# VectorE makes 12 of 16 k-tiles of the modulation sums for norm 1's last three k-tiles, in a backbone-layer kernel on one core

## The chip, the cores and the metric

The kernel runs on one core of one Trainium2 chip. TensorE (PE in the profile, PEld its weight loads) multiplies into PSUM; VectorE (DVE) and ScalarE (ACT) work on SBUF and PSUM; SyncE (SP) issues most DMAs. The metric is the device time of one execution in microseconds (us), lower is better; times are medians of runs on the chip.

## What is computed

One layer over 128 context tokens and 256 latent tokens, all in float32, with d = 2048: modulation vectors from two conditioning vectors, an RMS norm that they scale and shift, an input projection, attention and a Fourier branch, gates, an output projection, and a SwiGLU feed-forward part behind a second norm. Only the start matters here:

```python
def modulation(cond, w_mod, b_mod):
    m = jax.nn.silu(cond) @ w_mod + b_mod
    return jnp.split(m[..., None, :], 6, axis=-1)
...
    sh1, sc1, g1, sh2, sc2, g2 = modulation(cond, w_mod_l, b_mod_l)
    h = rms_norm(x, n1) * (1 + sc1) + sh1
    q, k, v, u = project_in(h, w_in_l, qg_l, kg_l)
```

`w_mod` is 2048 x 12288. Each of sh1 and sc1 is, for each of the two conditions, a sum over 2048 rows of the weight, that is over 16 k-tiles of 128 rows. The other four (g1, sh2, sc2, g2) are needed later.

## The kernel before

**Tiles and units.** Large products are made in float32r as three products of high and low halves (`mm3`, lines 146 to 149). Weights come in units of 256 x 512, loaded by SyncE into `wraw` (four buffers) and split into `wh` by ScalarE and `wl` by VectorE (`split`, lines 142 to 144). `next_unit` (208) splits a unit two ahead of the one that TensorE multiplies, and calls the paced side work in the lists `front` and `behind`: each `Paced` object (58) adds its `rate` to `due` at every unit and, once `due` reaches `least`, runs so many steps of its generator.

**The input projection** runs over k-tiles in four groups, `GROUPS` = (0, 1), (1, 2), (3, 4), (7, 9) (first k-tile, count), each over eight column blocks, so that multiplying can begin as soon as the first normed k-tile is there. A unit of the groups with 2 or 4 k-tiles is 18 products of 128 x 512 on TensorE; at the end of a block VectorE adds three PSUM tiles to `acc` (line 682). The 8 units of the group (1, 2) are called the second group below.

**The modulation of norm 1** is made for output k-tiles in groups, `MODS` = (0, 1), (1, 3), (4, 3), (7, 3), (10, 3), (13, 3). For a group of three, `mod_sums` (392) has 8 steps of two k-tiles of `w_mod`: four matmuls of 128 x 32 by 128 x 384 in plain float32, which lie in four column groups of the array (line 404), from `wm` tiles with four buffers (`mod_weights`, 376). In the trace each such matmul stands as two records, so a step is 8 records. Behind the last step ScalarE copies the sums to `mrow` (412), and `mod_cols` (416) turns them to columns by three small matmuls with `sel` (420) and three VectorE additions. Then `modulate` (535) makes h for one k-tile per step. `prepare` (570) runs the next group's sums with the steps behind the last group's sums in between (`next(follow, None)`, 577), at rates `PREP` = 1.75, 1.8, 1.8, 1.8 and `least` 3.6, that is, in bursts of three or four steps every second unit.

**The other modulation vectors** are made by VectorE alone (`mod_rows`, 306): two conditions times 16 k-tiles of `scalar_tensor_tensor` over 128 x 1024 (line 329), then a matmul with `ones` that adds up the partitions (338) into one of the four `at` buffers of PSUM, and an addition of the bias (343). This side work (`rows`) begins when `prepare` ends (`prep.then = with_rows`, 605) and goes on at fixed rates per unit through all later stages, to the feed-forward part. Attention's transposes (862, 865, 960), score and value products take their PSUM tiles from the same four `at` buffers in turn.

**Order.** The kernel runs under a manual schedule: each engine executes its instructions in the order in which the code emits them, and waits where a tile or a buffer is not ready.

Of the kernel before, what the change touches and what calls it, by code (L numbers as in the profile page):

```python
# [13 lines left out]
F32 = mybir.dt.float32  # L14
F32R = mybir.dt.float32r
AF = mybir.ActivationFunctionType
ALU = mybir.AluOpType
AX = mybir.AxisListType

P = 128  # L20
D = 2048
KT = D // P
# [17 lines left out]
GROUPS = [(0, 1), (1, 2), (3, 4), (7, 9)]  # L40
ORDER = [6, 7, 0, 1, 2, 3, 4, 5]
DUE = [-1.4, 0, 0, 0]
PREP = [1.75, 1.8, 1.8, 1.8]
PAIR = "t1 qk,b,,,,lq,s0 s1 m0,e0 i0,m1,pv lb,e1 i1,,t0,v,lv"


# [55 lines left out]
def trunk_kernel(ctx: ExitStack, tc: tile.TileContext, io: dict):  # L102
# [35 lines left out]
    def nm(s):  # L138
        return f"{s}{next(ids)}"
# [126 lines left out]
    with ExitStack() as ph:  # L266
# [22 lines left out]


        ROWS = (2, 4, 3, 5)

        def row_weights():

# [77 lines left out]
        def depth_of(n):  # L372

            return 4 if n == 1 else 2

        def mod_weights(alloc):


            def load(kt0, n, k0):
                w, nk = n * P, depth_of(n)  # L380
                wm = alloc([P, 2, nk, w], "wm")
                for ty in range(2):
                    col = ty * D + kt0 * P
                    nc.sync.dma_start(
                        wm[:, ty],
                        w_mod[k0 * P : (k0 + nk) * P, col : col + w].rearrange("(k p) n -> p k n", p=P),
                    )
                return wm

            return Ahead(load, [(kt0, n, k0) for kt0, n in MODS for k0 in range(0, KT, depth_of(n))], 0)  # L390

        def mod_sums(src, kt0, n, alloc, out):

# [3 lines left out]
            for k0 in range(0, KT, nk):  # L397
                _, wm = src.take()
                for kk in range(0, nk, 2):
# [13 lines left out]
                        out.append(rows)  # L413
                    yield

        def mod_cols(kt0, n, rows):

            pt = md_tile()
            for j in range(n):
                nc.tensor.matmul(pt[:, j * 4 : j * 4 + 4], rows[:, j * P : (j + 1) * P], sel, start=True, stop=True)  # L420
            m = pt[:, : n * 4].rearrange("p (k i c) -> p k i c", i=2, c=2)
            yield


            def bc(ap):
                return ap.unsqueeze(2).to_broadcast([P, n, 2])

            nc.vector.tensor_add(msh[0][:, kt0 : kt0 + n, :], m[:, :, 0], bc(bcol[:, kt0 : kt0 + n]))
            d = msc[0][:, kt0 : kt0 + n, :]
            nc.vector.tensor_add(d, m[:, :, 1], bc(bcol[:, KT + kt0 : KT + kt0 + n]))  # L430
            nc.vector.scalar_tensor_tensor(
                out=d, in0=d, scalar=1.0, in1=bc(ng[:, 0, kt0 : kt0 + n]), op0=ALU.add, op1=ALU.mult
            )
            yield


        with ExitStack() as pha:
            wmp = phm.enter_context(tc.tile_pool(name="wmp", bufs=4, side="right"))
            cpool = pha.enter_context(tc.tile_pool(name="cpool", bufs=12))
            tmp = pha.enter_context(tc.tile_pool(name="tmpa", bufs=2))  # L440

# [128 lines left out]
            def prepare():  # L570

                follow = columns_and_tokens(*MODS[0])
                while prepared[0] < 1:
                    yield next(follow)
                for k0, n in MODS[1:]:
                    for _ in mod_sums(src, k0, n, wme, sums):
                        next(follow, None)
                        yield
                    follow = columns_and_tokens(k0, n)
                    while k0 == 1 and prepared[0] < 3:  # L580
                        yield next(follow)
                for _ in follow:
                    yield

            prep = Paced(prepare())
            rows_psum["tile"] = md_tile

            def rows_and_columns():
# [62 lines left out]

            for gi, (k0, n) in enumerate(GROUPS):
                prep.due, prep.rate = DUE[gi], PREP[gi]
                prep.least = 3.6 if gi else 1
                if gi == len(GROUPS) - 1:
                    behind.append(Paced(expand_rpb(), 0.2))
                    new_ring()
# [755 lines left out]
```

## Time and profile before

| what | us |
|---|---|
| median of 3 runs | 2045.73 (2045.72 to 2048.85) |
| profiled execution, device time | 2046.09 |
| its span, first to last instruction | 2044.3 |
| TensorE busy in the span | 2022.1 |
| VectorE busy in the span | 1244.4 |

The span leaves out about 1.8 us around the instructions. TensorE's busy time is the union of its records, which overlap; idle time before a record stands in brackets in the views of the timeline, with what ended it. A wait that the profile names is put down to the semaphore that came last.

### The profile page before, as it was taken

What the parts mean: (1) busy time and instruction counts of PE and PEld (TensorE: products, weight loads), DVE (VectorE), ACT (ScalarE), POOL (GpSimd) and SP (SyncE); (2) the same over time, 40 slices, a digit from 0 to 9 for tenths busy, and PEclk for the clock granted to TensorE, in tenths of its full rate; (3) what the DMA queues carried; (4) which work ended last, traced back from release to release, by engine and by line L of the source; (5) the groups of instructions that cost most, each with busy time, mean ns of one, the idle gap of its engine ahead of it and who ended that gap; (6) DMA issues with size and microseconds to landing.
All of it is one profiled execution on the core that took longest, in us unless ns stands there. A gap on an engine that the chain in (4) does not pass through costs nothing.

```text
span 2044.3 us, 27532 instructions
## 1 busy us (share of the span) xinstructions
PE 2022.1 (99%) x10986; PEld 1844.3 (90%) x10986; DVE 1244.4 (61%) x1524; ACT 758.6 (37%) x1139; POOL 43.0 (2%) x92
## 2 busy tenths in 40 slices
PE   7999999999999999999999999999999999999999
PEld 4668888999999999889998999899989998999897
DVE  4746898778988778765844454544454334333456
ACT  5433232456656443334523332222322232323222
POOL 1000000000000000010000000000000000000000
PEclk8999999999999999999999999999999999999999
DMA  9995979677776776754455455444554444444453
GB/s 328 334 338 181 330 261 323 206 224 225 230 209 185 251 245 200 240 189 139 120 169 162 147 156 160 148 155 148 162 155 141 124 127 125 132 124 125 138 161 124
DMA packets 220384, 390.46 MB, mean 191 GB/s; under 512 B 28464, under 2 KB 77632, under 8 KB 220256
## 3 DMA queue, kind: packets, MB, share of 16 engines
q1 hardware_dynamic: 213088, 382.13, 59.5%
q10 hardware_dynamic: 4672, 6.31, 0.8%
q8 instruction: 86, 1.41, 0.3%
q0 software_dynamic: 2496, 0.27, 0.1%
q14 instruction: 42, 0.34, 0.0%
HBM read 371.81 MB, written 20.51 MB: 192 GB/s over the span
## 4 chain that ended last, share of the span: by engine, by line
PE 93%; DMA 3%; DVE 2%; ACT 1%; issue 0%; SPq 0%; ACTq 0%; DVEq 0%
PE mm L147 19%; PE mm L149 19%; PE mm L148 19%; PE at L147 11%; PE at L149 11%; PE at L148 11%; PE at L404 1%; DVE wl L144 1%; DMA wm<-in_w_mod 1%; DMA wraw<-in_w_in 1%; DVE accr L329 1%; DMA xc<-in_x_prompt 0%; PE at L981 0%; PE at L960 0%; PE at L338 0%
## 5 line engine op out<-in xcount | busy, mean ns | idle before, releaser
L144 DVE TENSOR_TENSOR wl<-wraw,wh 128x1024 fp32r<-128x1024 f32 (+1 forms) x464 | 559.1, 1205 | 672.7 <-ACT wh L143 668.9
L143 ACT CAST wh<-wraw 128x1024 fp32r<-128x1024 f32 (+1 forms) x464 | 481.1, 1038 | 1036.8 <-PE at L148 274.1
L147 PE MATMUL mm<-hH,wh 128*128 128x384 f32 x1152 | 387.9, 337 | 0.2 <-ACT gst L1036 0.2
L149 PE MATMUL mm<-hH,wl 128*128 128x384 f32 x1152 | 385.3, 334 | 0.0
L148 PE MATMUL mm<-hL,wh 128*128 128x384 f32 x1152 | 385.2, 334 | 0.0
L329 DVE SCALAR_TENSOR_TENSOR accr<-wmr,csz,accr 128x1024 f32<-128x1024 f32 x240 | 304.2, 1278 | 0.1
L147 PEld LDWEIGHTS mm<-hH,wh 128*128 128x128 f32 x1152 | 216.3, 188 | 5.1 <-issue 4.5
L148 PEld LDWEIGHTS mm<-hL,wh 128*128 128x128 f32 x1152 | 216.3, 188 | 0.0
L149 PEld LDWEIGHTS mm<-hH,wl 128*128 128x128 f32 x1152 | 216.2, 188 | 0.0
L147 PE MATMUL at<-hH,wh 128*128 128x384 f32 x640 | 213.9, 334 | 0.0
L149 PE MATMUL at<-hH,wl 128*128 128x384 f32 x640 | 213.9, 334 | 0.0
L148 PE MATMUL at<-hL,wh 128*128 128x384 f32 x640 | 213.8, 334 | 0.0
L147 PE MATMUL mm<-wh,hH 128*128 128x512 f32 x404 | 160.8, 398 | 1.9 <-ACT hH L548 1.2
L149 PE MATMUL mm<-wh,hL 128*128 128x512 f32 x404 | 158.4, 392 | 0.6 <-DVE hL L144 0.4
L148 PE MATMUL mm<-wl,hH 128*128 128x512 f32 x404 | 158.0, 391 | 0.8 <-DVE wl L144 0.8
L149 PE MATMUL mm<-wh,cL 128*128 128x512 f32 x352 | 137.1, 389 | 0.0
L147 PE MATMUL mm<-wh,cH 128*128 128x512 f32 x352 | 137.0, 389 | 0.0
L148 PE MATMUL mm<-wl,cH 128*128 128x512 f32 x352 | 137.0, 389 | 0.0
L147 PEld LDWEIGHTS at<-hH,wh 128*128 128x128 f32 x640 | 120.1, 188 | 1.0 <-ACT wh L143 0.8
L148 PEld LDWEIGHTS at<-hL,wh 128*128 128x128 f32 x640 | 120.1, 188 | 0.2
L149 PEld LDWEIGHTS at<-hH,wl 128*128 128x128 f32 x640 | 120.1, 188 | 0.0
L147 PEld LDWEIGHTS mm<-wh,hH 128*128 128x128 f32 x404 | 76.1, 188 | 25.6 <-issue 3.1
(282 smaller groups left out, 2631.1 us busy)
## 6 DMA issues: line engine op xcount, KB each, us to landing
wraw<-in_w_gate_up SPq DMA_DIRECT2D x176, 512.0 KB, 3.7
wmr<-in_w_mod SPq DMA_DIRECT2D x128, 512.0 KB, 4.9
wraw<-in_w_down SPq DMA_DIRECT2D x88, 512.0 KB, 3.7
wraw<-in_w_gate SPq DMA_DIRECT2D x64, 512.0 KB, 4.3
wm<-in_w_mod SPq DMA_DIRECT2D x80, 384.0 KB, 6.8
wraw<-in_w_in SPq DMA_DIRECT2D x56, 512.0 KB, 6.2
wraw<-in_w_o SPq DMA_DIRECT2D x32, 512.0 KB, 4.6
wraw<-in_w_fnet_proj SPq DMA_DIRECT2D x16, 512.0 KB, 5.0
```

Source lines behind the costliest of these rows:

```text
L143: nc.scalar.copy(H, x)
L144: nc.vector.tensor_sub(L, x, fr(H))
L147: nc.tensor.matmul(out, aH, bH, start=start, stop=False)
L148: nc.tensor.matmul(out, aH, bL, start=False, stop=False)
L149: nc.tensor.matmul(out, aL, bH, start=False, stop=stop)
L329: nc.vector.scalar_tensor_tensor(out=acc[:, cnd], in0=wm, scalar=sc, in1=acc[:, cnd], op0=ALU.mult, op1=ALU.add)
L404: nc.tensor.matmul(pm[q : q + 32, :w], csz[:, k, :], wm[:, ty, kk + par, :], start=k < 2, stop=k >= KT - 2, tile_position=(0, q), skip_gro ...
```

## The change

For the last group, (13, 3), the first four k-tiles (`EARLY` = 4) are still multiplied by TensorE. The other 12 k-tiles are multiplied and summed by VectorE in the new generator `late_sums`: for each k-tile and each of shift and scale one load of 128 x 384 (`wd`, five buffers) and two VectorE instructions over 128 x 384, one per condition, into four accumulators that lie in buffers of later h tiles. It is paced at `LATE` = 1.5 steps per unit from the second group of the projection on. `late_rows` then makes on TensorE the two remaining steps of sums and four matmuls with `hot`, which add the accumulators' partitions into the same PSUM tile. The steps behind the sums of (10, 3) no longer have the sums of (13, 3) in between: they come one after the other. The rates in the last two groups go from 1.8 to 1.6, and `least` from 3.6 to 1 in the last group and from the end of the sums of (10, 3) on.

```diff
-PREP = [1.75, 1.8, 1.8, 1.8]
+PREP = [1.75, 1.8, 1.6, 1.6]
+LATE = 1.5
+EARLY = 4
...
+        late_acc = []
+        hot = consts.tile([P, 2, 32], F32, tag="hot", name="hot")
+        nc.vector.memset(hot, 0.0)
+        for cnd in range(2):
+            nc.vector.memset(hot[:, cnd, cnd : cnd + 1], 1.0)
...
-            return Ahead(load, [(kt0, n, k0) for kt0, n in MODS for k0 in range(0, KT, depth_of(n))], 0)
+            return Ahead(load, [(kt0, n, k0) for kt0, n in MODS
+                for k0 in range(0, KT if kt0 < MODS[-1][0] else EARLY, depth_of(n))], 0)
...
+        def late_sums(kt0, n):
+
+            w = n * P
+
+            def load(k, ty):
+                wd = wdp.tile([P, w], F32, tag="wd", name=nm("wd"))
+                c0 = ty * D + kt0 * P
+                nc.sync.dma_start(wd, w_mod[k * P : (k + 1) * P, c0 : c0 + w])
+                return wd
+
+            for ty in range(2):
+                late_acc.append(
+                    [hpool.tile([P, w], F32, tag=f"t{c}{KT - 3 + ty}", name=nm("late")) for c in "HL"]
+                )
+            got = Ahead(load, [(k, ty) for k in range(EARLY, KT) for ty in range(2)], 5)
+            yield
+            for k in range(EARLY, KT):
+                for ty in range(2):
+                    if k + ty > EARLY:
+                        got.more()
+                    _, wd = got.take()
+                    for a, sc in zip(late_acc[ty], (csz[:, k, cnd : cnd + 1] for cnd in range(2))):
+                        if k == EARLY:
+                            nc.vector.tensor_scalar_mul(a, wd, sc)
+                        else:
+                            nc.vector.scalar_tensor_tensor(
+                                out=a, in0=wd, scalar=sc, in1=a, op0=ALU.mult, op1=ALU.add
+                            )
+                    yield
+
+        def late_rows(kt0, n, alloc, out):
+
+            w = n * P
+            pm = at_tile()
+            for k in range(0, EARLY, 2):
+                _, wm = src.take()
+                for ty in range(2):
+                    for par in range(2):
+                        q = 32 * (2 * ty + par)
+                        nc.tensor.matmul(
+                            pm[q : q + 32, :w], csz[:, k + par, :], wm[:, ty, par, :], start=k == 0, stop=False,
+                            tile_position=(0, q), skip_group_check=True,
+                        )
+            for ty in range(2):
+                for cnd, a in enumerate(late_acc[ty]):
+                    q = 32 * (2 * ty + cnd)
+                    nc.tensor.matmul(
+                        pm[q : q + 32, :w], hot[:, cnd], a, start=False, stop=True,
+                        tile_position=(0, q), skip_group_check=True,
+                    )
+            rows = alloc([P, w], "mrow")
+            nc.scalar.copy(rows, pm[:, :w])
+            out.append(rows)
...
+            wdp = phm.enter_context(tc.tile_pool(name="wdp", bufs=5, side="right"))
...
-                for k0, n in MODS[1:]:
+                for k0, n in MODS[1:-1]:
                     for _ in mod_sums(src, k0, n, wme, sums):
                         next(follow, None)
                         yield
                     follow = columns_and_tokens(k0, n)
                     while k0 == 1 and prepared[0] < 3:
                         yield next(follow)
-                for _ in follow:
+                prep.least = 1
+                yield from follow
+                while late.live:
+                    late.step()
                     yield
+                late_rows(*MODS[-1], wme, sums)
+                yield
+                yield from columns_and_tokens(*MODS[-1])
 
             prep = Paced(prepare())
+            late = Paced(late_sums(*MODS[-1]), LATE)
...
-                prep.least = 3.6 if gi else 1
+                prep.least = 3.6 if gi in (1, 2) else 1
+                if gi == 1:
+                    behind.append(late)
```

What this does to the order of instructions is shown at three places. In these rows L404, L420, L338, L329, L343 and L144 of the kernel before are L412, L482, L345, L336, L350 and L146 of the changed one; the number behind a name tells one tile from another.

On TensorE, where the last sums of the group (10, 3) stand, before (`at_1084` holds the sums of (10, 3), `at_1333` those of (13, 3)):

```order
L404 MATMUL at_1084<-wm_1154,csz 32x384 x4
L404 MATMUL at_1084<-wm_1164,csz 32x384 x4
L404 MATMUL at_1084<-wm_1178,csz 32x384 x4
L404 MATMUL at_1333<-wm_1192,csz 32x384 x4
L420 MATMUL at_1341<-sel,mrow_1277 128x4 x3
L404 MATMUL at_1333<-wm_1260,csz 32x384 x4
L404 MATMUL at_1333<-wm_1267,csz 32x384 x4
L404 MATMUL at_1333<-wm_1274,csz 32x384 x4
L404 MATMUL at_1333<-wm_1338,csz 32x384 x4
L404 MATMUL at_1333<-wm_1349,csz 32x384 x4
L404 MATMUL at_1333<-wm_1359,csz 32x384 x4
L404 MATMUL at_1333<-wm_1373,csz 32x384 x4
```

(36 products of units stand between the third and the fourth row, and between the eighth and the ninth.) The same place now (`at_1189` holds the sums of (10, 3), `at_1546` those of (13, 3)):

```order
L412 MATMUL at_1189<-wm_1281,csz 32x384 x4
L412 MATMUL at_1189<-wm_1295,csz 32x384 x4
L482 MATMUL at_1428<-sel,mrow_1426 128x4 x3
L463 MATMUL at_1546<-wm_1309,csz 32x384 x4
L463 MATMUL at_1546<-wm_1323,csz 32x384 x4
L470 MATMUL at_1546<-late_670,hot 32x384
L470 MATMUL at_1546<-late_671,hot 32x384
L470 MATMUL at_1546<-late_672,hot 32x384
L470 MATMUL at_1546<-late_673,hot 32x384
```

(54 products stand between the third and the fourth row.) Of the eight steps for (13, 3) two are left, and four single matmuls are new; the columns of (10, 3) stand directly behind that group's last sums, where a step of (13, 3) stood in between.

On VectorE, in the second group and behind it, at one of the units, before (`wl` is the low half of a unit, `acc` the projection's sums):

```order
L144 TENSOR_TENSOR wl_1041<-wraw_844,wh_1040 128x1024
L144 TENSOR_TENSOR wl_1065<-wraw_905,wh_1064 128x1024
L682 TENSOR_TENSOR acc_394<-acc_394,mm_1037 128x512
L682 TENSOR_TENSOR acc_394<-acc_394,mm_1038 128x512
L682 TENSOR_TENSOR acc_394<-acc_394,mm_1039 128x512
```

and the same stretch now:

```order
L146 TENSOR_TENSOR wl_1104<-wraw_887,wh_1103 128x1024
L449 SCALAR_TENSOR_TENSOR late_672<-wd_952,csz,late_672 128x384
L449 SCALAR_TENSOR_TENSOR late_673<-wd_952,csz,late_673 128x384
L146 TENSOR_TENSOR wl_1132<-wraw_956,wh_1131 128x1024
L449 SCALAR_TENSOR_TENSOR late_670<-wd_986,csz,late_670 128x384
L449 SCALAR_TENSOR_TENSOR late_671<-wd_986,csz,late_671 128x384
L449 SCALAR_TENSOR_TENSOR late_672<-wd_1069,csz,late_672 128x384
L449 SCALAR_TENSOR_TENSOR late_673<-wd_1069,csz,late_673 128x384
L754 TENSOR_TENSOR acc_401<-acc_401,mm_1100 128x512
L754 TENSOR_TENSOR acc_401<-acc_401,mm_1101 128x512
L754 TENSOR_TENSOR acc_401<-acc_401,mm_1102 128x512
```

Behind each `wl` two or four of the new instructions stand ahead of the additions that free the projection's PSUM tiles.

The third place lies much later, in the products of the two branches, where the sums of the fifth half of `mod_rows` end (`accr`; `gl` are gates, `hL` the low half of the mixed branches). `prepare` ends one unit later than before, and so all of `rows` stands about a unit later from there on. VectorE, before:

```order
L144 TENSOR_TENSOR wl_7155<-wraw_7021,wh_7154 128x1024
L329 SCALAR_TENSOR_TENSOR accr_6114<-wmr_7019,csz,accr_6114 128x1024
L1072 TENSOR_TENSOR gl_6944<-gl_6944,gl_6553 128x384
L144 TENSOR_TENSOR hL_1230_7160<-gl_6944,hH_1229_7159 128x384
L1072 TENSOR_TENSOR gl_6944<-gl_6944,gl_6553 128x384
L144 TENSOR_TENSOR hL_1232_7165<-gl_6944,hH_1231_7164 128x384
L144 TENSOR_TENSOR wl_7196<-wraw_7052,wh_7195 128x1024
L1072 TENSOR_TENSOR gl_6944<-gl_6944,gl_6553 128x384
L144 TENSOR_TENSOR hL_1237_7200<-gl_6944,hH_1236_7199 128x384
L1072 TENSOR_TENSOR gl_6944<-gl_6944,gl_6553 128x384
L144 TENSOR_TENSOR hL_1239_7205<-gl_6944,hH_1238_7204 128x384
L144 TENSOR_TENSOR wl_7236<-wraw_7086,wh_7235 128x1024
```

and now (`wl_7262` and `wl_7305` are what `wl_7196` and `wl_7236` were):

```order
L1144 TENSOR_TENSOR gl_7011<-gl_7011,gl_6619 128x384
L146 TENSOR_TENSOR hL_1253_7231<-gl_7011,hH_1252_7230 128x384
L146 TENSOR_TENSOR wl_7262<-wraw_7121,wh_7261 128x1024
L336 SCALAR_TENSOR_TENSOR accr_6189<-wmr_7119,csz,accr_6189 128x1024
L1144 TENSOR_TENSOR gl_7011<-gl_7011,gl_6619 128x384
L146 TENSOR_TENSOR hL_1259_7269<-gl_7011,hH_1258_7268 128x384
L1144 TENSOR_TENSOR gl_7011<-gl_7011,gl_6619 128x384
L146 TENSOR_TENSOR hL_1261_7274<-gl_7011,hH_1260_7273 128x384
L146 TENSOR_TENSOR wl_7305<-wraw_7152,wh_7304 128x1024
L336 SCALAR_TENSOR_TENSOR accr_6189<-wmr_7119,csz,accr_6189 128x1024
L146 TENSOR_TENSOR wl_7341<-wraw_7186,wh_7340 128x1024
```

The last addition to `accr` stood ahead of the gates' additions; now it stands behind all of them and behind two more splits, with one more addition to `accr` in between. On TensorE the matmul that reads this `accr`, before:

```order
L147 MATMUL mm_7153<-fH,wh_7113 128x384
L148 MATMUL mm_7153<-fL,wh_7113 128x384
L149 MATMUL mm_7153<-fH,wl_7114 128x384
L338 MATMUL at_7239<-accr_6114,ones 32x512 x4
L147 MATMUL at_7150<-fH,wh_7154 128x384
```

and now:

```order
L149 MATMUL mm_7219<-fH,wh_7220 128x384
L150 MATMUL mm_7219<-fL,wh_7220 128x384
L151 MATMUL mm_7219<-fH,wl_7221 128x384
L345 MATMUL at_7344<-accr_6189,ones 32x512 x4
L149 MATMUL at_7216<-fH,wh_7261 128x384
```

It stood ahead of the unit `wh_7154`, and stands ahead of the unit `wh_7261`, which was `wh_7195`: one unit of 24 products later.

## Rows read from the trace of the kernel before

**Rows 1.** The first lines of the page (busy time and share of the span of each engine) and the shares of the chain that ended last, by engine.

```profile
span 2044.3 us, 27532 instructions
...
PE 2022.1 (99%) x10986; PEld 1844.3 (90%) x10986; DVE 1244.4 (61%) x1524; ACT 758.6 (37%) x1139; POOL 43.0 (2%) x92
...
PE 93%; DMA 3%; DVE 2%; ACT 1%; issue 0%; SPq 0%; ACTq 0%; DVEq 0%
```

**Rows 2.** The waits of TensorE over the whole span: line <- what it waited for: us in total, times, longest. (L865 is a transpose of attention, L343 the addition of the bias to a row, L144 a split.)

```profile
PE at L865 <- DVE row L343: 1.2, 1, 1.2
PE at L420 <- ACT mrow L412: 0.9, 2, 0.6
...
PE at L865 <- DVE pt L144: 0.9, 1, 0.9
PE mm L148 <- DVE wl L144: 0.8, 1, 0.8
...
PE at L404 <- DMA wm<-in_w_mod: 0.4, 2, 0.2
```

**Rows 3.** The timeline of TensorE around one burst of three steps of sums in the third group: start, duration, line, operation, how many records.

```profile
126.75 0.39 PE L148 MATMUL mm<-wl,hH 128*128 128x512 f32 x1
126.97 0.39 PE L149 MATMUL mm<-wh,hL 128*128 128x512 f32 x1
127.29 2.14 PE L404 MATMUL at<-wm,csz 128*32 128x384 f32 x24
129.36 0.50 PE L147 MATMUL mm<-wh,hH 128*128 128x512 f32 x1
129.70 0.39 PE L148 MATMUL mm<-wl,hH 128*128 128x512 f32 x1
```

**Rows 4.** The timeline of TensorE where columns (420) stand directly behind the last sums of their own group; the idle time before a record, and what ended it, in brackets.

```profile
45.73 1.26 PE L404 MATMUL at<-wm,csz 128*32 128x384 f32 x8
47.57 0.83 PE L420 MATMUL at<-sel,mrow 128*128 128x4 f32 x6 [0.58 <-ACT mrow L412]
```

**Rows 5.** The table of stretches: the second group; from there to the last burst of sums; the modulation's end. Stretch, us, busy time (instructions) of PE, PEld, DVE, ACT, POOL, granted TensorE clock, busy share of the DMA engines, GB/s.

```profile
60.50:101.10 40.60, 40.52 (x248) 27.85 (x248) 27.83 (x42) 13.68 (x21) 0.00 (x0) 1.00 0.98 329
101.10:149.80 48.70, 48.70 (x289) 33.95 (x289) 22.54 (x33) 17.22 (x26) 0.00 (x0) 1.00 1.00 342
149.80:182.00 32.20, 32.20 (x166) 25.39 (x166) 18.20 (x26) 13.55 (x20) 2.48 (x5) 1.00 0.54 175
```

**Rows 6.** Groups of VectorE's instructions over the whole span: line, operation, out<-in, shapes, count | busy us, mean ns of one | idle time before them and what ended it.

```profile
L144 DVE TENSOR_TENSOR wl<-wraw,wh 128x1024 fp32r<-128x1024 f32 x448 | 548.1, 1224 | 671.9 <-ACT wh L143 668.3 <-DMA wraw<-in_w_in 2.8
L329 DVE SCALAR_TENSOR_TENSOR accr<-wmr,csz,accr 128x1024 f32<-128x1024 f32 x240 | 304.2, 1278 | 0.1
...
L327 DVE TENSOR_SCALAR accr<-wmr,csz 128x1024 f32<-128x1024 f32 x16 | 11.7, 747 | 0.0
...
L869 DVE SCALAR_TENSOR_TENSOR qL<-at,qg,qH 128x384 fp32r<-128x384 f32 x8 | 4.9, 609 | 0.0
```

**Rows 7.** The view of DMA from 60 to 150 us: GB/s in 40 equal slices, and the loads issued there (count, KB each, median us from issue to landing).

```profile
GB/s 157 219 350 384 376 313 351 306 373 382 385 370 349 379 269 233 337 322 362 393 387 362 368 376 268 214 355 339 384 379 339 303 334 374 342 279 288 315 386 377
...
wm<-in_w_mod SPq DMA_DIRECT2D x56, 384.0 KB, 6.5
wraw<-in_w_in SPq DMA_DIRECT2D x17, 512.0 KB, 6.3
```

**Rows 8.** The timeline of VectorE at the third place of the change (gates of the two branches).

```profile
737.84 1.22 DVE L144 TENSOR_TENSOR wl<-wraw,wh 128x1024 fp32r<-128x1024 f32 x1
738.97 1.28 DVE L329 SCALAR_TENSOR_TENSOR accr<-wmr,csz,accr 128x1024 f32<-128x1024 f32 x1
740.17 0.55 DVE L1072 TENSOR_TENSOR gl<-gl,gl 128x384 f32<-128x384 f32 x1
...
743.92 1.23 DVE L144 TENSOR_TENSOR wl<-wraw,wh 128x1024 fp32r<-128x1024 f32 x1 [0.40 <-ACT wh L143]
745.06 0.55 DVE L1072 TENSOR_TENSOR gl<-gl,gl 128x384 f32<-128x384 f32 x1
...
748.75 1.23 DVE L144 TENSOR_TENSOR wl<-wraw,wh 128x1024 fp32r<-128x1024 f32 x1 [0.39 <-ACT wh L143]
```

**Rows 9.** The timeline of TensorE at the same place: the matmul with `ones`, and products of the unit behind it.

```profile
745.11 1.06 PE L338 MATMUL at<-accr,ones 128*32 128x512 f32 x8
746.10 0.45 PE L147 MATMUL at<-fH,wh 128*128 128x384 f32 x1
...
746.75 0.34 PE L147 MATMUL at<-fH,wh 128*128 128x384 f32 x1
746.92 0.34 PE L148 MATMUL at<-fL,wh 128*128 128x384 f32 x1
```

**Rows 10.** The timeline of VectorE in attention, where a row's bias (343) stands ahead of attention's splits (`pt`).

```profile
481.14 1.23 DVE L144 TENSOR_TENSOR wl<-wraw,wh 128x1024 fp32r<-128x1024 f32 x1
482.28 0.69 DVE L969 TENSOR_TENSOR v<-vp,v 128x512 fp32r<-128x512 f32 x1
482.88 0.68 DVE L343 TENSOR_TENSOR row<-row,at 128x512 f32<-128x512 f32 x1
483.48 0.75 DVE L327 TENSOR_SCALAR accr<-wmr,csz 128x1024 f32<-128x1024 f32 x1
```

**Rows 11.** The timeline of TensorE at the same place.

```profile
481.93 0.49 PE L862 MATMUL at<-ident,qp 128*128 128x128 f32 x3
483.62 0.66 PE L865 MATMUL at<-ident,kp 128*128 128x128 f32 x4 [1.20 <-DVE row L343]
```

## The prediction, made before the changed kernel ran

> **What bounds the kernel now.** I read the head of the page first: TensorE is busy for 2022.1 of 2044.3 us, and the chain that ended last lies on it for 93% [rows 1]. VectorE has 61%, but that is a mean over stages. So a time comes from two things only: TensorE work taken away or added, and new idle time of TensorE. The second view is therefore its waits [rows 2]: they are few, and the longest that this change can touch has 1.2 us. Third, the table of stretches [rows 5]: from 60.5 to 149.8 us, where the change puts its work, TensorE has no gap worth naming, VectorE is busy for 27.8 of 40.6 us in the second group, and the DMA share is 0.98 to 1.00. There VectorE and the loads are the next bounds. Fourth, the timelines at the places where the order of instructions moves.
>
> **The change part by part.** Sums are made against the profiled execution's 2046.09 us, 0.36 above the median of 2045.73.
>
> *TensorE's steps.* Eight steps of sums become two, and four closing matmuls with `hot`, of the same shape as those of a step, are one more: five steps less. Three steps (24 records) run from 127.29 to 129.36, where the next product starts [rows 3]: 0.69 us a step, all of it on the path. 5 x 0.69 = **-3.45**.
>
> *Bursts.* Around a burst the products lose their pitch: 0.32 us from the last product's start to the burst and 0.34 from the first product's start to the next, where products follow at 0.22 or 0.23 [rows 3]. The order has one burst less: **-0.2**.
>
> *One by one.* Columns that stand directly behind their own sums wait for ScalarE's copy: 0.58 us, and the start lies 1.84 behind that of a burst that alone needs 1.26 [rows 4]. Before, a step of the next group stood in between nearly everywhere, and the two waits on `mrow` together are 0.9 [rows 2]. Now the columns of (10, 3) have no cover: **+0.6**. The columns of (13, 3) have a unit between them and their copy, and the steps of `modulate` are off TensorE; these cost nothing as long as h tiles are ready ahead of their units, which the planner asks for anyway.
>
> *VectorE in the second group.* 24 of the 48 new instructions lie there, four of them plain multiplications. No row has their form on this shape, so bounds: the 128 x 384 row that reads PSUM has 609 ns, and the 128 x 1024 row scaled by 384/1024 gives 0.48 [rows 6], less than that where records overlap, as 1.28 against the 1.20 to the next start does [rows 8]. I take 0.525, and 0.3 for a plain one (747 ns for 1024 [rows 6]): 20 x 0.525 + 4 x 0.3 = 11.7 us. With the 27.8 there, that is 39.5 of 40.6: VectorE is full. Each `wl` now stands behind two or four of these, up to 2.1 us, and the three additions that free the projection's PSUM tiles stand behind them too. Splits run two units ahead (a unit is over 4 us), which covers 2.1 but not a backlog. Bounds: 0, and 3.0 if the backlog grows to the sum of a bound of 0.609 for each (1.7 more) and of waits that hold VectorE up. I take **+0.7**, the size of the one wait on `wl` that exists [rows 2]. The other 24 lie in the third group, with 22.5 of 48.7 us busy [rows 5]: free. What VectorE would have made there is not delayed beyond its unit.
>
> *Loads.* The bytes are the same, but the 24 loads into `wd` (196 KB each, 4.7 MB) are issued earlier on SyncE's queue, ahead of units that TensorE needs; the two are even again in the third group. Before, 56 and 17 loads moved 30 MB in that time, at 329 and 342 GB/s with a DMA share of 0.98 to 1.00 [rows 5, 7], and TensorE waited 0.4 us for them in all [rows 2]. The best slices reach 384 to 393 GB/s [rows 7]. In 89.3 us the new order wants some 34.5 MB; four `wraw` buffers of 0.5 MB may come that much later: 32.4 MB, 363 GB/s. Between the mean and the best slices, nearer to these: 0 in the forecast; the other side is a rival. [...]
>
> *The fifth half of the rows.* `prepare` ends one unit later, so every later row step stands one unit later. At the third place this costs. Before, the last addition to `accr` started at 738.97 and ended at 740.25 [rows 8], and TensorE reads it at 745.11 [rows 9]: 4.9 us of slack. Now it stands behind the split that started at 748.75 [rows 8], with one more addition (1.20) ahead of it. It starts at 748.75 + 1.14 + 1.20 = 751.1 and ends at 752.4. TensorE is there one unit later, 24 products at 0.173 [rows 9]: 745.11 + 4.15 = 749.3. The wait is 3.1. No engine behind it can help, since TensorE works in order: **+3.1**; bounds 1.9 (the extra addition finds a gap) and 4.4 (another 1.2 of VectorE stands ahead of it).
>
> *Attention.* Its transposes and the rows share four `at` buffers. In two places TensorE waited for VectorE to free one, 1.2 and 0.9 [rows 2]. At 483.62 the row step's addition is what is late: it started at 482.88, behind a split and a `v` [rows 10, 11]. One unit later it stands behind those transposes, which then wait for `pt` as at the other place (0.9); the step itself, and those that make columns, fall on other transposes. One more wait of the size seen: **+1.2**; bounds -2.1 (both old ones vanish) and +3.3 (three more of 1.1).
>
> Sum: -3.45 - 0.2 + 0.6 + 0.7 + 3.1 + 1.2 = +1.95, so 2046.09 + 1.95 = **2048.0** us.
>
> **The rivals.** *B, the plain saving:* the row step at 745 and attention's waits cost no more than before, because VectorE drifts forward; against it is the order, which puts the last addition behind the split. Then -3.45 - 0.2 + 0.6 = -3.05: 2043.0.
>
> *C, the queue, on the slow side:* the loads don't come up to 363 GB/s. For it: the share of 1.00 at a mean of only 336; against it: TensorE hardly waited for them, so nobody asked for more, and the best slices. It decides below 363: at 350, 13 GB/s x 89.3 us = 1.2 MB, 3.3 us; at 336, 2.4 MB, 7.2 us. I take 4.3 more: 2052.3.
>
> *D, saving and old waits:* beyond B, the two waits of 1.2 and 0.9 vanish: 2040.9.
>
> *E, VectorE's price:* each multiply-add costs much more than 0.525, and the second group runs at VectorE's pace: at twice 0.525, 20 x 0.525 = 10.5 more in a stretch with 1.1 left, less 2 us of cover: about 2055. [...] The trace disagrees: L329 is such an instruction in float32, and takes 1278 ns where the split's plain tensor_tensor of that shape has 1224 [rows 6]. So it gets little.
>
> **How the numbers follow.** About 0.2% (4.1 us: below 2041.6 or above 2049.8) is what a measurement of this kernel can tell from no change. Forecast 0.57, with a range of 2044.3 to 2050.5 from the bounds of its terms, and about a sixth of it above 2049.8 (0.09). B 0.14, C 0.20, D 0.06, E 0.03. Faster: D, 0.06. Slower: C, E and 0.09: 0.32. The rest, 0.62, is the same. The range reaches from 2042.5, below B, to 2052.0, which takes in half of C: D, E and the other half of C stay out, with some ends of the others, 0.2. Predicted is the forecast's time.
>
> **What would show it.** In the profile of the changed kernel: two steps of sums in a burst, and one of four single matmuls, 0.69 us a step; a wait of L482 on `mrow` of about 0.6; on VectorE, L449 at about 0.52 a start, and a busy share near 1 between 60 and 101 us, with a wait of TensorE on `wl` or on a PSUM tile below 1 us; no wait of TensorE on `wraw` or `wm` above 0.5 us (else C); L345 near 749 us with about 3 us idle ahead of it for `accr` (if it has none, B); in attention, transposes that wait for `pt` or a row's or a column's tile, 3 us in all against 2.1. It is wrong if TensorE's idle time in the second group is above 3 us, or if row steps, which I moved by one unit from the order alone, meet VectorE elsewhere.

## The result

| | us |
|---|---|
| kernel before, median of 6 runs | 2046.06 (2045.06 to 2048.85) |
| changed kernel, median of 6 runs | 2055.29 (2051.8 to 2056.68) |
| ratio, 95% interval | 1.0041 (1.0032 to 1.0051) |
| changed kernel again, median of 5 runs (before: 2046.33) | 2053.73; 1.0035 (1.0022 to 1.0048) |
| profiled execution of the changed kernel | 2051.8, span 2049.9 |

Slower by 0.4%, and above the range. The profiled execution is the fastest of its six; it has 5.7 us more than that of before, and the medians differ by 9.2.

The changed kernel's page, first lines:

```profile
span 2049.9 us, 27535 instructions
...
PE 2021.9 (99%) x10946; PEld 1845.4 (90%) x10946; DVE 1269.9 (62%) x1575; ACT 757.3 (37%) x1139; POOL 43.6 (2%) x92
```

Its waits of TensorE (as [rows 2]):

```profile
PE at L345 <- DVE accr L336: 2.1, 1, 2.1
PE at L368 <- DVE pt L146: 2.0, 1, 2.0
PE at L345 <- DVE pt L146: 1.9, 1, 1.9
...
PE at L482 <- ACT mrow L420: 1.5, 3, 0.6
...
PE at L934 <- DVE pt L146: 0.8, 2, 0.4
PE mm L150 <- DVE wl L146: 0.8, 1, 0.8
...
PE mm L149 <- DVE acc L754: 0.2, 1, 0.2
PE at L412 <- DMA wm<-in_w_mod: 0.2, 1, 0.2
```

The two old waits in attention are gone and three of about 2 us are there; two stand on row matmuls (L345), one on the transpose that makes columns (L368). The second group itself is clean: TensorE has no wait there. The 0.2 for `acc` lies at 103 us, just behind it, and the 0.2 for `wm` ahead of 60 us. The table of stretches has the group's load (as [rows 5]):

```profile
60.50:101.10 40.60, 40.51 (x247) 27.60 (x246) 35.53 (x61) 13.35 (x20) 0.00 (x0) 1.00 1.06 376
```

The new instruction, in the groups of VectorE (as [rows 6]):

```profile
L449 DVE SCALAR_TENSOR_TENSOR late<-wd,csz,late 128x384 f32<-128x384 f32 x44 | 24.6, 612 | 0.1
```

The loads moved 376 GB/s where they had 329, at a share of 1.06. VectorE was busy for 35.5 of 40.6 us where it had 27.8; it wasn't full, since 20 of the 48 new instructions fell into this stretch (10.0 us) and not 24.

To see where the time goes I use four records that each trace has: columns near 48 us (in [rows 4]), the first Fourier product `at<-latH,uL` near 360, the last `at<-ident,sc` x8 of attention near 650, and the product near 814 that waits for `wl`. Between their starts lie the modulation and the projection; attention; the two branches' products. Behind the fourth each trace has 1225.6 or 1225.7 us to the start of the last matmul. The table has the us between these records, for all 14 traces. "Waits" are TensorE's of 1.9 us or more behind 60 us, "falls" the places behind 60 us at which the granted clock fell to 0.50 before the end.

| trace | to 360 | to 650 | to 814 | waits | falls |
|---|---|---|---|---|---|
| before | 313.11 | 289.35 | 163.84 | 0 | 0 |
| changed | 310.85 | 293.07 | 166.99 | 3 | 0 |
| changed, again | 312.02 | 294.62 | 166.96 | 3 | 1 |
| e1 rows back | 310.68 | 290.55 | 163.84 | 0 | 0 |
| e2 before, rows late | 314.61 | 296.22 | 167.00 | 3 | 2 |
| e3 late loads left out | 310.79 | 294.48 | 167.03 | 3 | 1 |
| e5 back behind attention | 310.79 | 295.96 | 167.66 | 3 | 3 |
| e6 back in attention | 310.69 | 289.54 | 168.47 | 1 | 1 |
| e7 rows earlier | 311.75 | 288.73 | 163.86 | 0 | 0 |
| e8 before, rows earlier | 314.27 | 289.29 | 163.94 | 0 | 0 |
| e9 row step first | 311.35 | 292.17 | 168.52 | 2 | 2 |
| e10 that and rows back | 310.70 | 288.55 | 163.83 | 0 | 0 |
| e11 e1, columns covered | 310.39 | 289.21 | 163.83 | 0 | 0 |
| e12 all three | 310.37 | 288.18 | 163.83 | 0 | 0 |

So the change does what it says: 2.3 us less in the first stage. Attention gives back 3.7 and the branches 3.15. What is left of the 5.7 lies ahead of the first record (48.25 us against 47.57) and in the last few tenths.

**Attention.** TensorE of the changed kernel at the two places (as [rows 11]):

```profile
478.49 0.82 PE L1032 MATMUL at<-ident,sc 128*128 128x128 f32 x6
...
480.33 0.66 PE L937 MATMUL at<-ident,kp 128*128 128x128 f32 x4
482.90 1.06 PE L345 MATMUL at<-accr,ones 128*32 128x512 f32 x8 [1.91 <-DVE pt L146]
...
628.91 0.60 PE L937 MATMUL at<-ident,kp 128*128 128x128 f32 x4
631.54 0.24 PE L368 MATMUL at<-ident,colr 32*128 32x32 f32 x1 [2.02 <-DVE pt L146]
```

and VectorE at the first (as [rows 10]):

```profile
480.42 1.23 DVE L146 TENSOR_TENSOR wl<-wraw,wh 128x1024 fp32r<-128x1024 f32 x1
481.56 0.69 DVE L1041 TENSOR_TENSOR v<-vp,v 128x512 fp32r<-128x512 f32 x1
482.16 1.02 DVE L146 TENSOR_TENSOR pt<-at,pt 128x512 fp32r<-128x512 f32 x2
```

Two tiles of `sc`, one of queries and one of keys take the four `at` buffers; the row's matmul is the fifth, and wants the first back. That one is freed by VectorE's `pt`, behind a `wl` and a `v`. TensorE has products of a whole unit behind L345 that need none of this, and still stood idle for 1.91 us ahead of it.

At the second place the transpose for the columns is the fifth user of the same four buffers, but what is late is not VectorE's queue. VectorE stands idle ahead of `pt`, and waits for ScalarE's half of it:

```profile
630.79 1.02 DVE L146 TENSOR_TENSOR pt<-at,pt 128x512 fp32r<-128x512 f32 x2 [3.21 <-ACT pt L145]
```

On ScalarE four DMA issues stand ahead of that half:

```profile
628.19 1.94 ACTq L1111 DMA_DIRECT2D s_gate<-gst  x4
630.17 0.86 ACT L145 CAST pt<-at 128x512 fp32r<-128x512 f32 x2 [1.56 <-PE at L937]
```

The profile puts ScalarE's wait down to a transpose of keys, whose last record starts at 629.24; ScalarE's issues end at 630.13. No run moved these issues, so their part is read from the order alone.

In all, the waits of attention are 1.9, 2.0, 0.8 (`pt`) and 0.6 (`gst`, ScalarE's copies out of PSUM) where they were 1.2, 0.9 and 0.2 (`gst`): 3.0 of the 3.7 us. The other 0.7 stands in no wait that the profile names.

**The branches.** TensorE near 750 us (as [rows 9]):

```profile
751.43 1.05 PE L345 MATMUL at<-accr,ones 128*32 128x512 f32 x4
754.58 1.05 PE L345 MATMUL at<-accr,ones 128*32 128x512 f32 x4 [2.10 <-DVE accr L336]
755.56 0.44 PE L149 MATMUL at<-fH,wh 128*128 128x384 f32 x1
```

and VectorE (as [rows 8]):

```profile
752.10 1.23 DVE L146 TENSOR_TENSOR wl<-wraw,wh 128x1024 fp32r<-128x1024 f32 x1 [0.39 <-ACT wh L145]
753.24 1.28 DVE L336 SCALAR_TENSOR_TENSOR accr<-wmr,csz,accr 128x1024 f32<-128x1024 f32 x1
```

The first condition's half runs, the second waits for the last addition: from 751.43 to the next product 4.13 us, where before it took 0.99.

**The clock.** The second trace of the changed kernel is 2.7 us longer than the first, 1.2 of it in the first stage and 1.55 in attention, and in attention it has a thing that the first lacks. In the first stage it is one tile of `wm` that came late, in a burst of four steps of sums. The burst of the first trace, and the product behind it:

```profile
122.61 2.44 PE L412 MATMUL at<-wm,csz 128*32 128x384 f32 x28
124.98 0.50 PE L149 MATMUL mm<-wh,hH 128*128 128x512 f32 x1
```

and of the second one:

```profile
122.59 2.51 PE L412 MATMUL at<-wm,csz 128*32 128x384 f32 x24
125.31 0.84 PE L412 MATMUL at<-wm,csz 128*32 128x384 f32 x4 [0.21 <-DMA wm<-in_w_mod]
126.07 0.50 PE L149 MATMUL mm<-wh,hH 128*128 128x512 f32 x1
```

The wait is named with 0.2, but the product stands 1.1 later; no other of the 14 traces has a wait for `wm` between 60 and 150 us. In attention it is the clock. The table of stretches there, first of the trace without the fall:

```profile
482.00:484.00 2.00, 1.10 (x9) 0.27 (x9) 2.00 (x5) 1.71 (x4) 0.00 (x0) 1.00 0.57 122
484.00:486.00 2.00, 2.00 (x12) 2.00 (x13) 2.00 (x4) 0.00 (x0) 0.00 (x0) 1.00 0.84 271
486.00:488.00 2.00, 2.00 (x14) 2.00 (x13) 1.69 (x3) 0.00 (x0) 0.69 (x2) 1.00 0.63 124
```

and of the second one:

```profile
482.00:484.00 2.00, 0.13 (x2) 0.00 (x0) 2.00 (x4) 2.00 (x7) 0.00 (x0) 0.89 0.04 8
484.00:486.00 2.00, 1.96 (x9) 0.30 (x9) 2.00 (x5) 0.86 (x1) 0.00 (x0) 0.50 0.86 277
486.00:488.00 2.00, 2.00 (x9) 2.00 (x10) 2.00 (x3) 0.00 (x0) 0.00 (x0) 0.75 0.53 128
```

At the same wait the granted clock (third column from the right) fell from 1.00 to 0.50: 0.11, 0.50 and 0.25 of 2 us each are 1.7 us of full clock lost. The stage itself is 1.55 longer, and that is the price to go by. Over all 14 traces 10 of 18 waits of 1.9 us or more have a fall at their end or right behind it, and no shorter wait behind 60 us has one (the longest is 1.27 us). It fits that the changed kernel's runs spread over 5 us, with mean clocks between 0.994 and 0.998, and that its median lies above its fastest, profiled run: three falls of 1.5 are 4.5 us. For the runs without a trace it isn't shown: one of 2053.18 us has a mean clock of 0.998.

### The profile page after: what moved, and what is told of

Read it like the earlier page. It is cut to its first block, busy times and chain, and to the rows that moved or that the text cites. A ratio compares the mean times of both kernels' runs of the same rounds, so it can differ in the third digit from the quotient of the medians.

```text
span 2049.9 us, 27535 instructions
## 1 busy us (share of the span) xinstructions
PE 2021.9 (99%) x10946; PEld 1845.4 (90%) x10946; DVE 1269.9 (62%) x1575; ACT 757.3 (37%) x1139; POOL 43.6 (2%) x92
## 4 chain that ended last, share of the span: by engine, by line
PE 90%; DMA 4%; DVE 3%; ACT 2%; issue 1%; SPq 0%; ACTq 0%; DVEq 0%
PE mm L149 18%; PE mm L151 18%; PE mm L150 18%; PE at L149 11%; PE at L151 11%; PE at L150 11%; DMA wm<-in_w_mod 1%; DVE wl L146 1%; DVE accr L336 1%; DMA wraw<-in_w_in 1%; PE at L412 1%; DMA bp<-s_rpb 1%; ACT wh L145 1%; DMA xc<-in_x_prompt 0%; PE at L345 0%
## 5 line engine op out<-in xcount | busy, mean ns | idle before, releaser
L146 DVE TENSOR_TENSOR wl<-wraw,wh 128x1024 fp32r<-128x1024 f32 (+1 forms) x464 | 559.3, 1206 | 666.5 <-ACT wh L145 664.8
L336 DVE SCALAR_TENSOR_TENSOR accr<-wmr,csz,accr 128x1024 f32<-128x1024 f32 x240 | 304.5, 1278 | 3.1 <-DMA wmr<-in_w_mod 2.8
```

What stands on the lines that cost most here:

```text
L146: nc.vector.tensor_sub(L, x, fr(H))
L336: nc.vector.scalar_tensor_tensor(out=acc[:, cnd], in0=wm, scalar=sc, in1=acc[:, cnd], op0=ALU.mult, op1=ALU.add)
```

## The experiments

My theory (A) was that the rows, late by one unit, cost the time; the rival (B) that the crowded second group does. Ratios are to the kernel before (medians of 2046.2 to 2046.4) on the same chip. Diffs are against the changed kernel, except e2 and e8.

**e1, rows back.** They missed one tick at 1.5:

```diff
-                behind.append(rows)
+                rows.due += 1.5; behind.append(rows)
```

> The changed kernel with one difference: the paced rows start with 1.5 steps in hand, the missed unit's share, so that every row's matmul with ones and both column transposes stand at the same product count on TensorE as in the kernel before. Theory A (the loss is the one unit by which the rows are late): the waits of L345 at 483 and 755 us (1.9 and 2.1 us) and of L368 at 632 (2.0) go, the two old waits of L935-like transposes in attention (1.2 and 0.9) come back, and the time falls by about 7 us (3.9 that attention lost in the trace, 3.1 at 755) to some 2045 in a trace like the first one, 2048 against a median of 2055.3. Theory B (the second group, its loads and VectorE, costs the time): it stays within 2 us of the changed kernel, at 2053 to 2056.

The median is 2045.04, the ratio 0.9994 (0.9985 to 1.0003). The three waits are gone, the old ones are back, and the branches have their 163.84 to the hundredth:

```profile
PE mm L149 <- ACT gst L1108: 1.4, 2, 1.3
...
PE at L937 <- DVE pt L146: 0.9, 1, 0.9
PE at L937 <- DVE row L350: 0.8, 1, 0.8
```

Attention is still 1.2 longer than in the kernel before. Most of that is the waits for `gst`: 1.4 here, and at most 0.8 in the other traces. Theory A holds, with 7.2 us between the profiled executions where it said about 7. The median went to 2045 and not to 2048: what had made the median of the changed kernel longer than its trace went too.

**e2, before with rows late.** The same line with `-= 1.5` in the kernel before.

> The kernel before with one difference: the paced rows start 1.5 steps in debt, so that every row's matmul and both column transposes stand at the same product count as in the changed kernel. The sums of (13, 3) stay on TensorE. Theory A: the waits of the changed kernel appear in attention and near 750 us, about 7 us slower than before: 2053. Theory B: no change, 2046.

The median is 2057.19, the ratio 1.0051 (1.0038 to 1.0063): more than A's 7 us. The three waits of the changed kernel stand there, without any of the late sums:

```profile
PE at L338 <- DVE accr L329: 2.4, 2, 2.1
...
PE at L361 <- DVE pt L144: 2.0, 1, 2.0
PE at L338 <- DVE pt L144: 1.9, 1, 1.9
```

Attention is 6.9 longer than before (296.22 less 289.35): the changed kernel's 3.7, and two falls of the clock at 1.6 each. The first stage is 1.5 longer, of which 1.3 stand at a row's matmul at 354 us, whose second half waits 0.3 for `accr`; A had neither term.

**e3, late loads left out.**

```diff
             def load(k, ty):
+                if one:
+                    return one[0]
                 wd = wdp.tile([P, w], F32, tag="wd", name=nm("wd"))
+                one.append(wd)
```

> The changed kernel with 23 of the 24 loads into wd left out (all multiply-adds read the first tile, so the sums of (13, 3) are other numbers): 4.5 MB less on the queue. Theory A: the same waits in attention and at 755, so within 1 us of the changed kernel in the trace, 2052 to 2055. Theory B, and the rival of the queue (unlucky runs in which the loads come late and TensorE waits): 3 us or more faster than the changed kernel in the median, and a mean clock of 0.997 in all runs.

The median is 2053.56, the ratio 1.0034 (1.0021 to 1.0047), with the same waits and one fall. Beside the next run's 2053.73, the loads cost nothing that the medians show. Theory B and the rival of the queue fall as the cause of the loss, since both wanted 3 us or more here.

**The changed kernel again.**

> The changed kernel again, for a second trace and more runs: the first trace has 2051.8 us, the median of its runs 2055.3, with mean clocks from 0.994 to 0.998. Theory A says that the trace's waits are there in every run, and that what lies above 2052 is spread of the first 60 us, where the clock is not yet full; theory B that slow runs have waits for wm, wraw or wl between 60 and 150 us that the first trace doesn't show.

The median is 2053.73. The trace's three waits are there. Between 60 and 150 us it has no wait for `wraw` or `wl`, but it has the one for `wm` at 125 us, so theory B got 1.1 of these 2.7 us. The other 1.55 are the clock's fall at 483 us, which neither theory had; the first 60 us, where A put the spread, are not longer (48.19 us to the first record, against 48.25).

**e5 and e6, one half each.** In e5 the 1.5 steps come back behind attention, in e6 the rows have them from the start and lose them there:

```diff
-        rows.rate = RATES[2]
+        rows.rate = RATES[2]; rows.due += 1.5
```

> The changed kernel with the rows late by one unit only up to the end of attention: they get the 1.5 steps back where the products of the branches begin, so that L345 near 750 us stands where it stood before. Theory A (two places, each with its own price): the wait of 2.1 us at 755 goes, those at 483 and 632 stay, with the falls of the clock behind them in some runs; 3.1 us below the changed kernel, 2050.6 to 2051. Rival (a step that comes earlier meets another wait, or the time is made good later): within 1 us of the changed kernel, 2053 to 2055.

The median is 2054.75, the ratio 1.0037 (1.0025 to 1.005): no gain, and A's number was wrong. The wait at 755 is gone, but a wait of its size took its place, where the extra steps fall. TensorE there:

```profile
694.34 0.34 PE L151 MATMUL mm<-aH,wl 128*128 128x384 f32 x1
696.63 0.44 PE L149 MATMUL mm<-aH,wh 128*128 128x384 f32 x1 [1.96 <-DVE gl L1169]
```

and VectorE:

```profile
679.29 4.87 DVE L336 SCALAR_TENSOR_TENSOR accr<-wmr,csz,accr 128x1024 f32<-128x1024 f32 x4
...
687.23 1.28 DVE L336 SCALAR_TENSOR_TENSOR accr<-wmr,csz,accr 128x1024 f32<-128x1024 f32 x1 [1.00 <-DMA wmr<-in_w_mod]
...
692.64 1.21 DVE L146 TENSOR_TENSOR wl<-wraw,wh 128x1024 fp32r<-128x1024 f32 x1
693.78 1.27 DVE L336 SCALAR_TENSOR_TENSOR accr<-wmr,csz,accr 128x1024 f32<-128x1024 f32 x1
694.97 1.01 DVE L146 TENSOR_TENSOR aL<-aT,aH 128x384 fp32r<-128x384 f32 x2
696.02 0.56 DVE L1169 TENSOR_TENSOR gl<-gl,mm 128x384 f32<-128x384 f32 x1
```

The gate addition that frees TensorE's PSUM tile stands behind one more `accr`: four in a row at 679 us, where the changed kernel's trace has three. The next `accr` then waits 1.0 for the load of its weights. Together that is 2.2 us. This trace has three falls of the clock, one of them at this wait.

> The other half: the rows have their old place up to the end of attention and are late by one unit from there on. Theory A: no wait of 1.9 or 2.0 us in attention and no fall of the clock there (mean clock 0.998 in every run), but the wait at 755; 3.1 us above the kernel with the rows back everywhere (2045.0), 2048.1. Rival (the fall of the clock comes from the wait at 755 or from the second group): clocks of 0.996 stay in some runs, 2050 and more.

The median is 2049.42, the ratio 1.0015 (1.0006 to 1.0023), 4.4 above e1 and 1.3 above A's number. Attention is clean (289.54), the wait at 751 is there, and its profile has a fall right behind it (0.90, 0.50 and 0.74 in three stretches of 2 us). So the fall isn't attention's alone, which is one half of what the rival said: the delay at this place has a price of its own of 3.1, and 1.5 more when the clock falls (168.47 against 166.99).

**e7 and e8, rows one unit earlier,** in the changed kernel (`+= 3.0`) and in that of before (`+= 1.5`).

> The changed kernel with rows that start with 3 steps in hand, one unit earlier than in the kernel before. Theory A: what a row step costs depends on the unit in which it falls, so the waits that are left in attention (0.8 on a row, 0.9 on pt) and the waits of the changed kernel are all gone or moved; if they are gone, 2043.4; if the earlier steps meet other transposes, up to 2048. Rival (rows have slack only in one direction, so earlier is free but gains nothing): 2045.

> The kernel before with rows that start one unit earlier than they did (1.5 steps in hand), the sums of (13, 3) on TensorE: the same places of the row steps as in the run with the changed kernel and earlier rows. Theory A: slower than that run by the saving of the sums alone, 1.3 to 2.4 us. Rival (the saving of TensorE's sums is not real, and the first study's 1.3 us between the medians is spread): the same within 0.5 us.

The medians are 2045.83 (0.9997, 0.9988 to 1.0006) and 2047.63 (1.0005, 0.9996 to 1.0015). With the rows at one place the late sums gain 1.8 us between these medians, and 1.3 between e1 and the kernel before. The earlier place trades the old waits for others of 0.3 to 0.7 (a column's transpose for `sc`), and gains nothing by it, as the rival said.

**e9 and e10, the row step first.** In attention's units the rows' step is emitted ahead of attention's; e10 has e1's line too.

```diff
-        front += [br_work, rows]
+        front += [rows, br_work]
```

> The changed kernel, rows one unit late as in it, but in the feed of attention the step of the rows is emitted ahead of attention's step of the same unit and not behind it. Theory A (the 1.9 and 2.0 us are the price of standing behind four transposes that fill all four at buffers): the waits at 483 and 632 us go, with the falls of the clock behind them; what is left there is a transpose that waits for the row's addition (about 1 us at 483); the wait of 2.1 at 755 stays. 3 to 5 us below the changed kernel: 2050. Rival (VectorE is late in those units whatever stands first): the waits move to the transposes in the same size, 2054.

The median is 2051.67, the ratio 1.0024 (1.0014 to 1.0035). The two waits of attention are gone with the rows as late as before; TensorE at the first place is now

```profile
484.17 1.06 PE L345 MATMUL at<-accr,ones 128*32 128x512 f32 x8
...
487.22 0.66 PE L937 MATMUL at<-ident,kp 128*128 128x128 f32 x4 [0.85 <-DVE pt L146]
```

It stays above 2050: in its trace the swap has made a wait of 1.94 (0.75 in the changed kernel) for the Fourier branch's `uL` at 374, now behind one more `accr`, and the clock fell there and at 756.

> The same swap with the rows at the place of the kernel before. Theory A: no wait at 755 and none of 2 us in attention; the small ones there (0.8 on a row, 0.9 on pt) may move: within 1.5 us of the run with the rows back, 2044 to 2046.5. Rival: as there, up to 2048.

The median is 2043.32, the ratio 0.9985 (0.9976 to 0.9994): 3.0 us faster than the kernel before, with runs from 2042.6 to 2044.0. Attention's trace is 2.0 shorter than e1's; 0.8 is the wait for the row, and another 0.8 is less waiting for `gst`, which nothing here ties to the swap.

**e11, columns covered, and e12, all three.**

```diff
-                prep.least = 1
+                prep.least, prep.due = 1, 0; yield
```

Both have the rows' line with `+= 3.0`, and e12 the swap too.

> The kernel with the rows back, and the columns of (10, 3) one unit behind their sums instead of directly behind them (the rows get one unit more in hand, so that they keep the place of before). The prediction's term: the wait of L482 on mrow at 139 us (0.6) goes, 0.6 us below the kernel with the rows back, 2044.4. Rival (the products behind wait for h or for a burst instead): 2045 or more.

The median is 2044.33, the ratio 0.9991 (0.9983 to 1.0). L482 no longer waits there, which is 0.3 in the trace's first stage; the 0.7 between this median and e1's is within their spread.

> All that helped in one kernel: the changed kernel with the rows at the place of before, the row step ahead of attention's step, and the columns of (10, 3) one unit behind their sums. If the terms add up (1.3 below the kernel before for the rows back, 1.7 for the swap, 0.6 for the columns), 2042.7. Rival (the columns' 0.6 is lost again in a wait of the next stage): 2043.3, as without them.

The median is 2043.2, the ratio 0.9987 (0.9978 to 0.9996): as e10. The trace is the shortest of all (span 2040.3 against 2041.0), the medians don't tell the two apart.

## Why the prediction was wrong

- *TensorE's steps, bursts, columns, VectorE in the second group:* -2.35 in the sum, -2.26 in the trace. Other pairs of traces with the rows at one place give -2.43 (e1 and before), -2.52 (e7 and e8), -2.6 and -3.8 (the changed kernel's two and e2). Two steps and the closing one take 2.07, as three steps did:

```profile
152.71 1.50 PE L463 MATMUL at<-wm,csz 128*32 128x384 f32 x16
154.03 0.83 PE L470 MATMUL at<-late,hot 128*32 128x384 f32 x8
154.78 0.50 PE L149 MATMUL mm<-wh,hH 128*128 128x512 f32 x1
```

  The new columns wait 0.6. VectorE's term was too dear, 0.2 to 0.4 where I took 0.7, and "VectorE is full" was wrong: 35.5 of 40.6 us.
- *Loads, and the rivals C and E:* C and E are wrong by the traces. 376 GB/s were to be had when asked for; the forecast's 0 for the loads holds in the first trace, and 1.1 at 125 us in the second. The multiply-add on 128x384 takes 612 ns, as the row of that shape that reads PSUM (609 [rows 6]), and not E's 1050 (twice 0.525 us).
- *The fifth half of the rows:* +3.1, measured 3.15. The order and the rows gave this one. (I had one wait of 3 us ahead of L345; the trace has its first half in time and a wait of 2.1 ahead of the second, with the same end.)
- **The step that failed is attention:** +1.2, bounds -2.1 to +3.3, measured +3.7, before any clock. I had the place (the row step falls behind the transposes) and the wrong victim: I let the transposes wait for `pt` and priced that with the 0.9 of the other place. In fact they waited 0.4 at most, and the row's matmul, the fifth user of four buffers, waited 1.9. The columns' transpose is the fifth user too, at 631.5, and waited 2.0, there behind ScalarE's half of `pt`: in the trace it stands two units (48 products) later, not one, and I had left it in "other transposes". That the row's shift alone makes these waits is shown by e1 and e2; e9 shows that it takes the order of the two steps within the unit.
- **A term was missing:** the clock. 10 of 18 waits of 1.9 us or more had a fall to 0.50 behind them, and a fall went with some 1.5 us more (1.55 and 1.48 where it stands alone in its stage); the changed kernel has three such waits, the kernel before none. With attention at 3.7 the sum would be 2050.5, and the profiled 2051.8 lies within the range; the median lies outside it, and what the traces show above the first one is the fall (1.55) and the late `wm` (1.1).
- The rival that said "slower" for another reason (C) had the sign and not the cause. E had the time, 2055, and not the cause.

What stays open: what decides whether a given wait has a fall behind it. The same wait at 483 us has one in one trace of the changed kernel and none in the other. Open too is how much of the 9.2 us between the medians the falls make, since only two executions of the changed kernel have a trace.

## What to carry to other kernels

Where side work is paced by units, an edit at 100 us that ends one unit later moves everything paced behind it, and the price falls due at 480, 630 and 750 us, not where the edit was made; give the phase back (one line here) before judging the edit. In a schedule like this one, price a moved step by who holds its buffer at the new place, by counting turns through the buffers and by what stands ahead of the release on each engine, not by a wait seen at another place. And here, with TensorE busy for 99% of the span, a wait of 2 us cost some 1.5 more in some executions (1.55 at 483 us) and nothing more in others.

## What the runs showed of the hardware

The granted clock fell to 0.50 in the middle of a kernel that is 99% busy, behind 10 of 18 single waits of 1.9 to 2.1 us, and the stage was about 1.5 us longer for each (1.55 in attention of the changed kernel's two traces, 1.48 in the branches of e6). Waits of 1.3 us or less behind 60 us never had it in 14 traces.
